# Three edits to a one-core hybrid decoder block in fp32: GpSimd's low parts of the weights in pieces, the last down product by columns, the first norm's weights spread on chip

## The chip, the cores and the metric

The kernel runs on one core of a Trainium2 chip. The metric is device time in microseconds, as the median of several runs of the whole program.

## The reference

One decoder block over 16 learned meta tokens and 256 tokens of 1024 numbers, in fp32, cut to what matters here:

```python
u = rmsnorm(h, norm_mix)                      # h: 272 x 1024
proj = u @ w_in                               # 1024 x 6160
y_ssd = ssd_branch(z, xbc, dt_raw, ...)       # Mamba-2 scan, convolution over 4 tokens
y_sc = short_conv_branch(gate_b, gate_c, hh)  # gated convolution over 3 tokens
h = h + concat(y_ssd, y_sc) @ w_out           # 2048 x 1024
u2 = rmsnorm(h, norm_ffn)
h = h + hier_moe(u2, ...)                     # 16 experts, two per token: (silu(t@Wg) * (t@Wu)) @ Wd
out = rmsnorm(h, norm_final)[:, 16:]
```

## The kernel before

The order of the instructions on each engine is the order of the code: nothing reorders it. The weights come through a ring of 22 tiles of 1 MB (`slot`), later 3 more, loaded by SP's queue in the order of use (`load`).

**Start.** SP's queue loads the meta tokens, the first 128 tokens of x in two halves, `norm_mix` twice (`gmt` for the meta tokens, `gmix` spread over 128 partitions, 512 KB), the second 128 tokens of x, the columns of dt (`wdt`) and then the tiles of `w_in`, with up to three small parameter loads (`between`) behind each. `u_squares`, `u_root` and `u_scale` make the norm of one row block, `u_turn` and `u_low` transpose it on TensorE and split it in a high part `uh` and a low part `ul`. `x_part` copies x into the four accumulators `acc[b][n]` (token block b, columns n) in PSUM, where the output product is added later.

**Projection.** `units` lists dt and 48 products of 128 columns of `w_in`. An fp32 product is made of three fast ones, (high, high), (low, high), (high, low), in `project`. `split_hi` (ScalarE, L313) and `split_lo` (L324) make a unit's weight parts two units ahead; the low part is one subtraction of 128x1024, on GpSimd for 24 of the units (`on_pool`) and on VectorE for the others. Behind a product `first` and `second` do convolution and gates on VectorE and ScalarE: L593 and L617 are taps of the convolutions, L602 and L605 gates, L504 to L515 the decay of the scan. TensorE's products use two PSUM banks ("pj") in turn, so a product waits until `first` has read the one two before.

**Experts.** Seven units, six of two experts and the last of four; each makes gate, up and down products (L1038), and its results are scattered into the accumulators (L1059). Weights are loaded when `used` frees a tile. Of the last expert tiles the second halves come in pieces: the first 1024 columns, then twice 512, for the four experts in turn (L114 to L120).

**End.** The last unit's down product makes both halves of 512 columns for each k-block in turn; then come the scatters (the first 512 columns in a high and a low part, the other 512 in fp32, L1251), the squares, the roots and the norm (`last_norm`), and six output transfers. The weights of the last norm are spread on chip in the last unit (`fin_part`, L1066).

## Time and profile before

| | |
|---|---|
| median of 3 runs | 448.89 us (448.59 to 450.16) |
| the profiled execution | 448.21 us, span 446.2 |
| busy: TensorE, VectorE, ScalarE, GpSimd | 422.9, 229.9, 159.4, 66.2 us |
| mean granted TensorE clock | 0.993 of 2.4 GHz |
| read from HBM | 138.26 MB, 312 GB/s over the span |

The span goes from the first to the last instruction of the profiled execution; the small rest lies around it. A busy time is the sum over the engine's instructions, overlaps counted once. TensorE's matmuls are pipelined and their ends are modelled, so its busy time says less than its waits do. Rows of a timeline begin with the start and the duration in us; in square brackets stands how long the engine was idle before, and what ended that.

### The profile page before, as it was taken

How to read it: one execution, taken by the hardware profiler on the slowest of the kernel's cores; microseconds unless marked ns; L12 is line 12 of the kernel's file. 1: busy time of each engine (PE TensorE's matmuls, PEld its weight loads, DVE VectorE, ACT ScalarE, POOL GpSimd, SP SyncE). 2: the span in 40 equal slices, each digit the busy share in tenths (PEclk: the TensorE clock that was granted, in tenths of full speed). 3: DMA queues.
4: the chain of work that ended last, by engine and by line, in shares of the span. 5: the costliest groups of instructions: out<-in, count | busy, mean ns of one | idle time of the engine just before them, and what ended most of it. 6: DMA issues, size and time to landing. Idle time of an engine off the chain costs nothing.

```text
span 446.2 us, 7338 instructions
## 1 busy us (share of the span) xinstructions
PE 422.9 (95%) x2905; PEld 295.3 (66%) x2905; DVE 229.9 (52%) x472; ACT 159.4 (36%) x252; POOL 66.2 (15%) x39
## 2 busy tenths in 40 slices
PE   6999999999998999999999989999999999999982
PEld 4899899999997899978878353533535335353321
DVE  5679888977896858676556621110212102122113
ACT  4675446745757345554452321010010100101113
POOL 1253324244437242100000000000000000000000
PEclk9999999999999999999999999999999999999998
DMA  7999988265699556599684799999999999999952
GB/s 201 256 272 348 348 260 291 89 188 162 208 390 385 178 189 222 182 424 387 200 298 175 309 419 413 419 419 420 418 422 416 421 419 419 420 416 421 411 202 98
DMA packets 49468, 139.85 MB, mean 313 GB/s; under 512 B 6406, under 2 KB 32918, under 8 KB 37398
## 3 DMA queue, kind: packets, MB, share of 16 engines
q1 hardware_dynamic: 49142, 138.94, 82.9%
q8 instruction: 25, 0.41, 0.4%
q10 hardware_dynamic: 288, 0.39, 0.2%
q14 instruction: 13, 0.11, 0.1%
HBM read 138.26 MB, written 1.06 MB: 312 GB/s over the span
## 4 chain that ended last, share of the span: by engine, by line
PE 75%; DVE 14%; ACT 3%; SPq 3%; DMA 2%; issue 1%; ACTq 0%; DVEq 0%
PE gu L1038 22%; PE yd L1038 11%; PE acc L345 10%; PE p_c L337 5%; PE xp L1111 4%; PE p_xs L337 3%; PE p_h L337 3%; PE acc L1059 3%; PE p_z L337 3%; PE p_b L337 3%; DVE cv L593 2%; DVE h L617 2%; DVE f L324 1%; SPq L96 1%; DMA w<-in_w_in 1%
## 5 line engine op out<-in xcount | busy, mean ns | idle before, releaser
L1038 PE MATMUL gu<-w,X 128*64 128x512 f32 (+1 forms) x512 | 100.4, 595 | 0.4 <-DVE X L1078 0.4
L313 ACT ACTIVATE f<-w 128x1024 fp32r<-128x1024 f32 x64 | 67.2, 1054 | 30.8 <-PE acc L345 13.0
L324 POOL TENSOR_TENSOR f<-w,f 128x1024 fp32r<-128x1024 f32 x24 | 60.0, 2501 | 110.1 <-ACT f L313 93.6
L1038 PEld LDWEIGHTS gu<-w,X 128*64 128x64 f32 (+1 forms) x512 | 31.1, 130 | 60.2 <-issue 58.0
L324 DVE TENSOR_TENSOR f<-w,f 128x1024 fp32r<-128x1024 f32 x40 | 50.9, 1273 | 14.7 <-ACT f L313 14.6
L1038 PE MATMUL yd<-w,hd 128*64 128x512 f32 (+1 forms) x256 | 49.6, 595 | 0.5 <-DVE hd L1048 0.5
L345 PE MATMUL acc<-f,h 128*128 128x512 f32 x192 | 44.8, 391 | 0.0
L345 PEld LDWEIGHTS acc<-f,h 128*128 128x128 f32 x192 | 35.5, 188 | 7.7 <-issue 0.4
L1208 DVE TENSOR_TENSOR hb<-hb,gu 128x512 f32<-128x512 f32 x7 | 4.8, 687 | 64.3 <-PE gu L1038 62.2
L1054 DVE SCALAR_TENSOR_TENSOR Yl<-yd,ws,Yh 128x512 fp32r<-128x512 f32 x12 | 9.0, 751 | 53.6 <-PE yd L1038 38.5
L1038 PEld LDWEIGHTS yd<-w,hd 128*64 128x64 f32 (+1 forms) x256 | 15.2, 130 | 29.2 <-issue 27.6
L1053 ACT ACTIVATE Yh<-yd,ws 128x512 fp32r<-128x512 f32 x12 | 8.3, 688 | 73.4 <-PE yd L1038 56.7
L337 PE MATMUL p_b<-uh,f 128*128 128x256 f32 x128 | 16.6, 282 | 2.6 <-DVE h L605 1.9
L1111 PEld LDWEIGHTS <-hh 128*128 128x128 bf16 x192 | 18.1, 147 | 1.6 <-issue 1.6
L1111 PE MATMUL xp<-P,hh 128*128 128x128 bf16 x192 | 19.0, 225 | 0.0
L1111 PE MATMUL xp<-P,h 128*128 128x128 bf16 x96 | 16.9, 228 | 1.7 <-ACT hb L1192 1.7
L337 PE MATMUL p_xs<-uh,f 128*128 128x272 f32 x128 | 18.0, 293 | 0.1
L337 PE MATMUL p_c<-uh,f 128*128 128x258 f32 x128 | 16.9, 284 | 1.1 <-DVE h L605 1.1
L337 PEld LDWEIGHTS p_b<-uh,f 128*128 128x128 f32 x128 | 15.6, 188 | 3.4 <-issue 3.0
L1030 ACT ACTIVATE PT<-ptp 128x256 fp32r<-128x256 f32 x7 | 2.7, 384 | 42.2 <-PE ptp L1026 42.2
L1192 ACT ACTIVATE hb<-gu 128x512 f32<-128x512 f32 x7 | 4.2, 594 | 37.0 <-PE gu L1038 37.0
L337 PE MATMUL p_h<-uh,f 128*128 128x258 f32 x128 | 16.9, 285 | 0.0
(332 smaller groups left out, 664.3 us busy)
## 6 DMA issues: line engine op xcount, KB each, us to landing
w<-in_expert_w_gate SPq DMA_DIRECT2D x32, 1024.0 KB, 12.1
w<-in_expert_w_up SPq DMA_DIRECT2D x32, 1024.0 KB, 14.2
w<-in_expert_w_down SPq DMA_DIRECT2D x28, 1024.0 KB, 12.0
w<-in_w_in SPq DMA_DIRECT2D x23, 1024.0 KB, 7.3
w<-in_w_out SPq DMA_DIRECT2D x8, 1024.0 KB, 11.4
abc<-adr SPq DMA_DIRECT2D x2, 1024.0 KB, 5.7
w<-in_expert_w_down SPq DMA_DIRECT2D x4, 512.0 KB, 16.2
w<-in_expert_w_down SPq DMA_DIRECT2D x8, 256.0 KB, 6.3
```

The lines of the kernel that those rows point to most:

```text
L313: A.activation(h, src, AF.Copy)
L324: (G if on_pool(name, c) else V).tensor_tensor(l, src, h.bitcast(F32), op=OP.subtract)
L337: T.matmul(p, st_[:, k, :], mv[:, k, t0:], start=(k == 0 and st_ is terms[0][0] and mv is uh), stop=(k == KT - 1 and mv is ul))
L345: T.matmul(acc[b][n], st_[:, 128 * b:128 * (b + 1)], mv[:, 512 * n:512 * (n + 1)], start=False, stop=False, skip_group_check=True)
L593: V.scalar_tensor_tensor(s[:, lo:], p[:, o - sh + lo:o - sh + n], cw[:, 3 - sh, ft:ft + 1], s[:, lo:], op0=OP.mult, op1=OP.add)
L617: V.scalar_tensor_tensor(y, cc[:, c, 2 - sh:258 - sh], scw[:, 2 - sh, t:t + 1], y, op0=OP.mult, op1=OP.add)
L1038: T.matmul(o[c * s:c * s + c], X[:, 128 * k + c * s:128 * k + c * s + c], ws_, start=first_, stop=last_, tile_position=(0, c * s))
L1053: A.activation(Yh, y, AF.Copy, scale=ws)
L1054: V.scalar_tensor_tensor(Yl, y, ws, Yh.bitcast(F32), op0=OP.mult, op1=OP.subtract)
L1059: T.matmul(acc[b][n], PT[:, 128 * b:128 * (b + 1)], part, start=False, stop=stop and part is Y[-1], skip_group_check=True)
L1111: T.matmul(p[:, i], hparts[j][b].rearrange("p (m k) -> p k m", k=KT)[:, 4 * q + i], P[:, b], start=(j == b == 0), stop=(j == 2 and b == 1))
L1208: V.tensor_mul(hb, hb, g)
```

## The change

- **Low parts.** Where GpSimd makes a low part, it does so in four instructions of 128x256.
- **Start.** x is loaded in two transfers of 512 KB, right behind the meta tokens; the small loads stand behind other weight tiles than before. `norm_mix` comes as 128x8 numbers (`gcol`), issued by ScalarE; VectorE makes a diagonal pattern of them and TensorE spreads it with a matrix of ones into two of the accumulators (`g_spread`), from which `u_scale` reads. The copies of x into these two (`x_part`) follow behind the first and the second product. GpSimd zeroes `f0`, which VectorE did, and some of VectorE's constants are made later.
- **End.** The last down product is made in three column pieces (`THIRDS`), with the scatters and squares of the first 512 columns between; the norm's weights are loaded spread (`fin`) behind the three tiles of the second ring; the norm takes 512 columns at a time, and ScalarE's queue issues the four output transfers.

```diff
+THIRDS = [(0, 512), (512, 256), (768, 256)]
...
-                    for a in between[:3]:
+                    few = {(0, 1): 2, (1, 0): 6}.get((j, i), 2 * (j > 5))
+                    for a in between[:few]:
                         nc.sync.dma_start(*a)
-                    del between[:3]
+                    del between[:few]
...
-    fcol = cp.tile([128, KT], F32, name="fcol")
+    fin = cp.tile([128, D], F32, name="fin")
...
-    gmix = sA[:, 0:1024]
+    gdiag, gcol, all1 = sA[:, 0:1024], sA[:, 1568:1576], sA[:, 1600:1728]
...
+    A.dma_start(gcol, raw(norm_mix, 0, [[KT, 128], [1, KT]]))
+    A.dma_start(gmt, raw(norm_mix, 0, [[0, 16], [128, 8], [1, 128]]))
     for b in range(2):
-        for n in range(2):
-            nc.sync.dma_start(xt[:, b, 512 * n:512 * n + 512], raw(x, 128 * D * b + 512 * n, [[D, 128], [1, 512]]))
-        if b == 0:
-            nc.sync.dma_start(gmt, raw(norm_mix, 0, [[0, 16], [128, 8], [1, 128]]))
-            nc.sync.dma_start(gmix, raw(norm_mix, 0, [[0, 128], [1, D]]))
+        nc.sync.dma_start(xt[:, b], raw(x, 128 * D * b, [[D, 128], [1, D]]))
     nc.sync.dma_start(wdt, raw(w_in, 3072, [[6160, 128], [128 * 6160, KT], [1, 16]]))
...
+    between += [(dtb[:16], raw(dt_bias, 0, [[1, 16], [1, 1]])), (alog, raw(A_log, 0, [[0, 128], [1, 16]]))]
     between += [(pr[a:a + n, :], row(p, n)) for p, a, n in (
         (ssd_conv_b, 0, 16), (ssd_conv_w, 16, 64), (sc_conv_w, 80, 24), (ssd_norm, 104, 8), (sc_norm, 112, 8),
         (norm_ffn, 120, 8))]
-    between += [(dtb[:16], raw(dt_bias, 0, [[1, 16], [1, 1]])), (alog, raw(A_log, 0, [[0, 128], [1, 16]])),
-                (dsk, raw(D_skip, 0, [[1, 2], [2, 8]])), (gf, raw(norm_ffn, 0, [[KT, 128], [1, KT]])),
-                (fcol, raw(norm_final, 0, [[KT, 128], [1, KT]])),
+    between += [(dsk, raw(D_skip, 0, [[1, 2], [2, 8]])), (gf, raw(norm_ffn, 0, [[KT, 128], [1, KT]])),
                 (wgr, raw(router_group_w, 0, [[4, 128], [512, KT], [1, 4]])),
...
+    V.memset(zero, 0.0)
+    f0 = slot("f0").bitcast(F32R)
+    G.memset(all1, 1.0)
+    G.tensor_copy(f0[:, 0:1024], zero.to_broadcast([128, 1024]))
...
+    def g_spread():
+        V.tensor_tensor(gdiag.rearrange("p (m k) -> p m k", k=KT), idt[:, :, None].to_broadcast([128, 128, KT]),
+                        gcol[:, None].to_broadcast([128, 128, KT]), op=OP.mult)
+        for n in range(2):
+            T.matmul(gp[n], all1, gdiag[:, 512 * n:512 * n + 512], start=True, stop=True)
+    gp = acc[0][1], acc[1][0]
     def u_squares(b):
         un[b] = un01[:, 1024 * b:1024 * b + 1024]
-        for n in range(2):
-            c = slice(512 * n, 512 * n + 512)
-            A.activation(un[b][:, c], xt[:, b, c], AF.Square, accum_out=norms[:, 3 * n + b:3 * n + b + 1])
+        A.activation(un[b], xt[:, b], AF.Square, accum_out=norms[:, 3 + b:4 + b])
     def u_root(b):
         rr[b] = r = norms[:, b:b + 1]
-        V.tensor_scalar(r, r, 1.0 / D, EPS, op0=OP.mult, op1=OP.add)
-        A.activation(r, norms[:, 3 + b:4 + b], AF.Sqrt, bias=r, scale=1.0 / D)
+        A.activation(r, norms[:, 3 + b:4 + b], AF.Sqrt, bias=eps, scale=1.0 / D)
     def u_scale(b):
         V.reciprocal(rr[b], rr[b])
         for n in range(2):
             c = slice(512 * n, 512 * n + 512)
-            V.scalar_tensor_tensor(un[b][:, c], xt[:, b, c], rr[b], gmix[:, c], op0=OP.mult, op1=OP.mult)
+            V.scalar_tensor_tensor(un[b][:, c], xt[:, b, c], rr[b], gp[n], op0=OP.mult, op1=OP.mult)
...
-        (G if on_pool(name, c) else V).tensor_tensor(l, src, h.bitcast(F32), op=OP.subtract)
+        if on_pool(name, c):
+            for k in range(0, KT, 2):
+                G.tensor_tensor(l[:, k:k + 2], src[:, k:k + 2], h[:, k:k + 2].bitcast(F32), op=OP.subtract)
+        else:
+            V.tensor_tensor(l, src, h.bitcast(F32), op=OP.subtract)
...
-    V.tensor_copy(f0, zero.to_broadcast([128, 2048]))
-    V.tensor_add(stack, idt[:32, 0:16], idt[:32, 16:32])
     t = {}
     m_sums()
+    g_spread()
     x_part(0, 0)
+    m_scale()
     u_squares(0)
     u_root(0)
-    m_scale()
-    x_part(0, 1, 0, 256)
+    u_squares(1)
+    u_root(1)
+    mean = bp.tile([128, 2, 32], F32, name="mean")
+    V.memset(mean[:, 0], 1.0 / 256)
+    V.memset(mean[:, 1], 0.0)
+    V.memset(mean[0:64, 1, 0:16], 1.0 / 64)
+    V.memset(mean[64:128, 1, 16:32], 1.0 / 64)
+    V.tensor_scalar(upper, jp, 0.0, None, op0=OP.is_ge)
+    V.tensor_scalar(nupper, jp, 0.0, -1.0, op0=OP.is_ge, op1=OP.mult)
+    V.tensor_scalar(below, jp, 0.0, None, op0=OP.is_lt)
+    sup = bp.tile([128, 128], BF, name="sup")
+    V.tensor_scalar(sup, jp, 0.0, None, op0=OP.is_gt)
+    V.tensor_add(stack, idt[:32, 0:16], idt[:32, 16:32])
     mp = m_turn()
-    x_part(0, 1, 256, 512)
     u_scale(0)
     m_low(mp)
-    u_squares(1)
-    u_root(1)
     for q in range(2):
         t[0, q] = u_turn(0, q)
-    x_part(1, 0)
     x_part(1, 1)
...
+            if i in (0, 1):
+                x_part(i, 1 - i)
...
+            nc.sync.dma_start(fin, raw(norm_final, 0, [[0, 128], [1, D]]))
...
-    def fin_part(q, tag):
-        p = bank(tag, "fp")
-        for i in range(4):
-            T.matmul(p[:, 128 * i:128 * i + 128], on1, dg[:, 4 * q + i], start=True, stop=True)
-        V.tensor_copy(fin.rearrange("p (m k) -> p k m", k=KT)[:, 4 * q:4 * q + 4],
-                      p.rearrange("p (k m) -> p k m", k=4))
...
-                    left[1, 1] = [lambda: fin_part(0, "pj")]
-                    left[1, 3] = [lambda: fin_part(1, "m")]
...
-    Y0 = [wk.tile([128, 512], F32R, name=n, tag=n) for n in ("Yh", "Yl")]
-    Y1 = ff[:, 0:512]
-    A.activation(Y0[0], ys[0], AF.Copy, scale=ws)
-    V.scalar_tensor_tensor(Y0[1], ys[0], ws, Y0[0].bitcast(F32), op0=OP.mult, op1=OP.subtract)
-    for n in range(2):
-        A.activation(Y1[:, 256 * n:256 * n + 256], ys[1][:, 256 * n:256 * n + 256], AF.Copy, scale=ws)
-    for b in range(2):
-        scatter(b, 0, PT, Y0[0:1])
+    oo = slot("o", free.pop(0)).rearrange("p (b d) -> p b d", b=2)
+    Y1 = wk.tile([128, 512], F32, name="Y1", tag="X")
+    Y = [wk.tile([128, 512], F32R, name="Yh", tag="Yh"), slot("Y", free.pop(0)).bitcast(F32R)[:, 0:512]]
+    def squares_of(b, n):
+        A.activation(oo[:, b, 512 * n:512 * n + 512], acc[b][n], AF.Square, accum_out=s4[:, b, n:n + 1])
+    for i, tag in enumerate(("m", "m", "pj")):
+        c, n = THIRDS[i]
+        y = bank(tag, "yd")[:, :n]
+        for k in range(4):
+            side_by_side(y, hd, w_of(u, 2, k, c, n), k, k == 0, k == 3)
+        if i == 0:
+            weighed(y, ws, Y)
+        elif i == 1:
+            A.activation(Y1[:, 0:256], y, AF.Copy, scale=ws)
+            for part in Y:
+                for b in range(2):
+                    scatter(b, 0, PT, [part], part is Y[1])
+            for b in range(2):
+                squares_of(b, 0)
+        else:
+            V.tensor_scalar(Y1[:, 256:512], y, ws, None, op0=OP.mult)
+    used(2 * ne)
     for b in range(2):
...
     def last_norm():
-        squares_of(0, 0)
-        first_sum(0)
-        squares_of(0, 1)
-        root(0)
-        V.reciprocal(s3[:, 0:1], s3[:, 0:1])
-        for n in range(2):
-            squares_of(1, n)
-        norm_part(0, 0, 256)
-        first_sum(1)
-        root(1)
-        norm_part(0, 256, 256)
-        norm_part(0, 512, 512)
-        V.reciprocal(s3[:, 1:2], s3[:, 1:2])
-        norm_part(1, 0, 512)
-        norm_part(1, 512, 256)
-        norm_part(1, 768, 256)
+        for b in range(2):
+            first_sum(b)
+        for b in range(2):
+            squares_of(b, 1)
+            root(b)
+        for b in range(2):
+            V.reciprocal(s3[:, b:b + 1], s3[:, b:b + 1])
+            for n in range(2):
+                c = slice(512 * n, 512 * n + 512)
+                V.scalar_tensor_tensor(oo[:, b, c], acc[b][n], s3[:, b:b + 1], fin[:, c], op0=OP.mult, op1=OP.mult)
+                A.dma_start(raw(out, b * 128 * D + 512 * n, [[D, 128], [1, 512]]), oo[:, b, c])
```

SP's queue at the start, before (`sA` and `xt` take the meta tokens, `norm_mix` and x, `w_` a tile of `w_in`, `sB`, `sC` and `dtb` small parameters):

```order
L167 DMA sA<-in_meta_tokens 128x128
L170 DMA xt<-in_x 128x512 x2
L172 DMA sA<-in_norm_mix 128x1x128
L173 DMA sA<-in_norm_mix 128x1024
L170 DMA xt<-in_x 128x512 x2
L174 DMA sB<-in_w_in 128x8x16
L92 DMA w_112<-in_w_in 128x8x128
L96 DMA sB<-in_ssd_conv_b 16x128
L96 DMA sB<-in_ssd_conv_w 64x128
L96 DMA sB<-in_sc_conv_w 24x128
L92 DMA w_112<-in_w_in 128x8x128
```

and changed:

```order
L170 DMA sA<-in_meta_tokens 128x128
L174 DMA xt<-in_x 128x1024 x2
L175 DMA sB<-in_w_in 128x8x16
L93 DMA w_110<-in_w_in 128x8x128 x2
L98 DMA dtb<-in_dt_bias 16x1
L98 DMA sC<-in_A_log 128x16
L93 DMA w_115<-in_w_in 128x8x256
L98 DMA sB<-in_ssd_conv_b 16x128
L98 DMA sB<-in_ssd_conv_w 64x128
```

Both loads of `norm_mix` have left this queue, x is whole behind the meta tokens, and the second weight tile stands ahead of the rows of `ssd_conv_b` and the like.

TensorE at the start, before (`acc_68` to `acc_71` are the accumulators, `up` the transposed norm, `p_dt` and `p_B` the first products, `prp` the transposed parameters):

```order
L251 MATMUL acc_71<-norms,sA 128x1
L271 MATMUL acc_68<-xt,idt 128x512
L271 MATMUL acc_69<-xt,idt 128x256
L261 MATMUL acc_71<-idt,sA 128x128
L271 MATMUL acc_69<-xt,idt 128x256
L279 MATMUL up<-idt,un 128x128 x8
L271 MATMUL acc_70<-xt,idt 128x512
L271 MATMUL acc_71<-xt,idt 128x512
L279 MATMUL up<-idt,un 128x128 x8
L337 MATMUL p_dt_264<-uh,f_155 128x272 x8
```

and changed:

```order
L248 MATMUL acc_71<-norms,sA 128x1
L228 MATMUL acc_69<-sA 128x512
L228 MATMUL acc_70<-sA 128x512
L268 MATMUL acc_68<-xt,idt 128x512
L258 MATMUL acc_71<-idt,sA 128x128
L276 MATMUL up<-idt,un 128x128 x8
L268 MATMUL acc_71<-xt,idt 128x512
L276 MATMUL up<-idt,un 128x128 x8
L339 MATMUL p_dt_258<-uh,f_137 128x272 x8
L339 MATMUL p_dt_258<-ul,f_137 128x272 x8
L268 MATMUL acc_69<-xt,idt 128x512
L431 MATMUL prp<-idt,sB 128x128
```

Two matmuls that spread `norm_mix` (L228) have come in ahead, and one copy of x has moved behind p_dt; another stands behind the first p_B.

TensorE in the last down product, changed, at the end of its second column piece:

```order
L1050 MATMUL yd<-w_3799,hd 32x256
L1050 MATMUL yd<-w_3801,hd 32x256
L1071 MATMUL acc_68<-Yh,PT 128x512
L1071 MATMUL acc_70<-Yh,PT 128x512
L1071 MATMUL acc_68<-Y,PT 128x512
L1071 MATMUL acc_70<-Y,PT 128x512
L1050 MATMUL yd<-w_3689,hd 32x256
L1050 MATMUL yd<-w_3691,hd 32x256
```

All four scatters of the first 512 columns stand ahead of the third piece, where they stood behind the whole product.

## Rows read from the trace of the kernel before

**Rows 1.** Two stretches: busy time by engine, granted clock, DMA share, GB/s.

```profile
9.45:12.90 3.45, 3.08 (x10) 2.44 (x11) 2.55 (x7) 2.91 (x8) 0.00 (x0) 0.51 0.72 160
...
300.00:360.00 60.00, 60.00 (x348) 25.54 (x348) 10.61 (x21) 5.14 (x9) 0.00 (x0) 1.00 1.01 419
```

**Rows 2.** TensorE's waits, 27 to 200 us: total, times, longest.

```profile
PE p_b L337 <- DVE h L605: 1.9, 1, 1.9
PE p_c L337 <- DVE h L605: 1.1, 1, 1.1
PE yp L529 <- DVE h L515: 1.0, 1, 1.0
PE p_b L337 <- DVE h L602: 0.7, 1, 0.7
PE p_B L337 <- ACT sC L611: 0.7, 1, 0.7
```

**Rows 3.** The page's group of GpSimd's low parts (busy, mean ns, idle before).

```profile
L324 POOL TENSOR_TENSOR f<-w,f 128x1024 fp32r<-128x1024 f32 x24 | 60.0, 2501 | 110.1 <-ACT f L313 93.6
```

**Rows 4.** VectorE's timeline (start, duration, line, operation, tiles, count), 128 to 140 us.

```profile
128.86 3.14 DVE L617 SCALAR_TENSOR_TENSOR h<-h,col,h 128x256 f32<-128x256 f32 x2
...
133.38 1.00 DVE L617 SCALAR_TENSOR_TENSOR h<-h,col,h 128x256 f32<-128x256 f32 x2
...
135.77 1.53 DVE L617 SCALAR_TENSOR_TENSOR h<-h,col,h 128x256 f32<-128x256 f32 x1
...
137.33 2.47 DVE L617 SCALAR_TENSOR_TENSOR h<-h,col,h 128x256 f32<-128x256 f32 x1
```

**Rows 5.** GpSimd's timeline, 134 to 141 us.

```profile
134.85 2.16 POOL L554 TENSOR_TENSOR h<-h 128x512 f32<-128x512 f32 x1 [3.66 <-ACT h L550]
136.97 2.55 POOL L324 TENSOR_TENSOR f<-w,f 128x1024 fp32r<-128x1024 f32 x1
139.49 1.46 POOL L554 TENSOR_TENSOR h<-h 128x512 f32<-128x512 f32 x1
```

**Rows 6.** GpSimd's last low part, and TensorE's product that uses it.

```profile
178.17 2.40 POOL L324 TENSOR_TENSOR f<-w,f 128x1024 fp32r<-128x1024 f32 x1 [4.81 <-ACT f L313]
...
181.42 2.06 PE L337 MATMUL p_b<-uh,f 128*128 128x256 f32 x16
```

**Rows 7.** The start: timelines of SP's queue, ScalarE, VectorE and TensorE.

```profile
5.99 4.07 SPq L96 DMA_DIRECT2D sB<-in_ssd_conv_b  x1
...
9.54 0.63 ACT L236 ACTIVATE un<-xt 128x512 f32<-128x512 f32 x1 [1.95 <-DMA xt<-in_x]
...
9.02 1.42 DVE L247 SCALAR_TENSOR_TENSOR un<-xt,norms,sA 128x512 f32<-128x512 f32 x2 [2.11 <-DMA sA<-in_norm_mix]
...
9.82 1.97 PE L279 MATMUL up<-idt,un 128*128 128x128 f32 x8 [2.11 <-DVE un L247]
...
13.94 1.04 PE L279 MATMUL up<-idt,un 128*128 128x128 f32 x8
...
15.23 1.28 PE L337 MATMUL p_dt<-uh,f 128*128 128x272 f32 x8 [0.25 <-ACT uh L280]
```

**Rows 8.** The end: TensorE, SP's last weight issue with its landing, VectorE's last.

```profile
417.55 1.16 PE L1066 MATMUL fp<-fin,o 128*128 128x128 f32 x8
...
426.13 0.33 SPq L120 DMA_DIRECT2D w<-in_expert_w_down  x1
...
w<-in_expert_w_down SPq DMA_DIRECT2D x1, 256.0 KB, 5.3
...
427.68 7.07 PE L1038 MATMUL yd<-w,hd 128*32 128x512 f32 x64 [0.52 <-DVE hd L1048]
...
434.78 0.74 PE L1059 MATMUL acc<-Yh,PT 128*128 128x512 f32 x2
...
436.85 1.02 PE L1251 MATMUL acc<-fin,PT 128*128 128x256 f32 x4
...
439.92 1.53 DVE L1258 SCALAR_TENSOR_TENSOR o<-acc,s,fin 128x512 f32<-128x512 f32 x3
```

More of the change, by code (lines that the diff above doesn't have):

```diff
@@ L210, in body @@
     V.memset(nones, -1.0)
-    f0 = slot("f0").bitcast(F32R)
     G.iota(count16, pattern=[[1, NE]], base=0, channel_multiplier=0, allow_small_or_imprecise_dtypes=True)
     G.iota(sl, pattern=[[1, CAP]], base=-1024, channel_multiplier=0, allow_small_or_imprecise_dtypes=True)
-    mean = bp.tile([128, 2, 32], F32, name="mean")
-    V.memset(mean[:, 0], 1.0 / 256)
-    V.memset(mean[:, 1], 0.0)
-    V.memset(mean[0:64, 1, 0:16], 1.0 / 64)
-    V.memset(mean[64:128, 1, 16:32], 1.0 / 64)
-    V.tensor_scalar(upper, jp, 0.0, None, op0=OP.is_ge)
-    V.tensor_scalar(nupper, jp, 0.0, -1.0, op0=OP.is_ge, op1=OP.mult)
-    V.tensor_scalar(below, jp, 0.0, None, op0=OP.is_lt)
-    sup = bp.tile([128, 128], BF, name="sup")
-    V.tensor_scalar(sup, jp, 0.0, None, op0=OP.is_gt)
     uh = up.tile([128, KT, L], F32R, name="uh")
@@ L1192, in body @@
                 A.activation(hb, g, AF.Silu)
-                if last:
-                    ff = slot("fin", free.pop(0))
-                    dg, fin = ff[:, 0:1024].rearrange("p (k m) -> p k m", k=KT), ff[:, 1024:2048]
-                    oo = slot("o", free.pop(0)).rearrange("p (b d) -> p b d", b=2)
-                    on1 = oo[:, 0, 0:128]
-                    V.memset(on1, 1.0)
-                    V.tensor_tensor(dg, idt[:, None].to_broadcast([128, KT, 128]),
-                                    fcol[:, :, None].to_broadcast([128, KT, 128]), op=OP.mult)
-                    left[1, 1] = [lambda: fin_part(0, "pj")]
-                    left[1, 3] = [lambda: fin_part(1, "m")]
                 if not last:
@@ L1219, in body @@
             P = Pn
+        if last:
+            break
         ys = [bank("m", "yd") for n in range(2)]
@@ L1222, in body @@
             for y, (c, n) in zip(ys, HALVES):
-                side_by_side(y[:, 0:n], hd, w_of(u, 2, k, c, n), k, k == 0, k == 3)
+                side_by_side(y, hd, w_of(u, 2, k, c, n), k, k == 0, k == 3)
             if k % 2:
                 used(ne)
-        if last:
-            break
         Y = weighed(ys[0], ws)
@@ L1238, in body @@
         left[0, 3] = [lambda b=b, PT=PT, k=keep: scatter(b, 1, PT, k[0]) for b in range(2)]
[L1241 to L1248 removed]
+    oo = slot("o", free.pop(0)).rearrange("p (b d) -> p b d", b=2)
[7 more added lines that the diff above has]
+        for k in range(4):
+            side_by_side(y, hd, w_of(u, 2, k, c, n), k, k == 0, k == 3)
+        if i == 0:
[10 more added lines that the diff above has]
+    used(2 * ne)
     for b in range(2):
@@ L1252, in body @@
                      Y1[:, 256 * c:256 * c + 256], start=False, stop=True, skip_group_check=True)
-            if b == 0:
-                scatter(c, 0, PT, Y0[1:], True)
-    def norm_part(b, c0, w):
-        c = slice(c0, c0 + w)
-        V.scalar_tensor_tensor(oo[:, b, c], acc[b][c0 // 512][:, c0 % 512:c0 % 512 + w], s3[:, b:b + 1], fin[:, c],
-                               op0=OP.mult, op1=OP.mult)
-        (A if c0 == 512 else nc.sync).dma_start(raw(out, b * 128 * D + c0, [[D, 128], [1, w]]), oo[:, b, c])
-    def squares_of(b, n):
-        A.activation(oo[:, b, 512 * n:512 * n + 512], acc[b][n], AF.Square, accum_out=s4[:, b, n:n + 1])
     def first_sum(b):
@@ L1293, in body @@
         over()
+        for b in range(2):
+            squares_of(b, 0)
         last_norm()
```

1 line of the change is left out of this document (removed).

## The prediction

> **What bounds the kernel now.** I read the stretches first, then who waits for whom on TensorE, then the lines behind each wait. In the expert part TensorE has no free time while the DMA engines run at 419 GB/s [rows 1]: both are full, so what follows 250 us moves only if its start moves. Before it, from 27 to 200 us, TensorE's waits are few: five of 0.7 us or more, together 5.4, every one but the last behind VectorE [rows 2]. So there are three places where time can be had: the start, these waits, and what follows the last matmul.
>
> The profiled execution takes 448.21 us (span 446.2), 0.68 under the median of the runs shown, 448.89. I make the sum against the former and take it from the latter.
>
> **GpSimd's low parts.** GpSimd makes 24 low parts of 1024 columns at 2.5 us on average [rows 3]. What they do to VectorE is in its own rows: two L617 take 1.00 us together when GpSimd is idle, 3.14 when they meet a low part, and in the next unit 1.53 for one and 2.47 for the other [rows 4]. The instruction itself needs 0.5; the rest ends when a GpSimd instruction ends (134.85 + 2.16 = 137.0 and 136.97 + 2.55 = 139.5, [rows 5]). So the two share a way into memory, and a GpSimd instruction keeps it to its end. The same rows show how it is handed over: GpSimd had its next instruction ready at 136.97 without a pause, yet the first L617 still came through by 137.30, and GpSimd's low part took 2.55 in place of 2.40 [rows 5]. A waiting VectorE instruction gets in between two GpSimd instructions.
>
> Cut into four, a piece should take 2.40 / 4 = 0.6 plus a fixed part. The row of 512 columns gives it: 1.46 against 2.40 / 2 = 1.20, at most 0.26 [rows 5]. So 0.6 to 0.86 a piece, 0.7 taken; a wait of up to 2.4 becomes one of at most 0.7 for each VectorE instruction. Then:
> - The wait of 1.9 us on L605 [rows 2] lies behind the L617 of 2.47 [rows 4]: that one falls to about 0.5 + 0.5, so 1.5 comes back there, and the earlier unit's pair (3.14) brings 1.0 more. I take all of 1.9.
> - The 0.7 on L602 lies behind the pair of 3.14: gone.
> - The 0.7 of p_B on ACT belongs to the start, below.
> - The 1.0 on L515 and the 1.1 on p_c stay. Ahead of each VectorE has a chain of instructions that read two operands from SBUF or copy within it (L496 and the twelve of L504 to L506; L566 to L568); each of them meets a piece of its own, so four short waits replace a long one and VectorE ends no sooner.
>
> That is 1.9 + 0.7, less 0.1 for what new waits take: **2.5 us**. Bounds: 0, if VectorE never gets in between, and 4.7, if the 1.0 and 1.1 go too. The Trainium skill (SBUF — State Buffer, § Who interferes with whom) says that the pair of ports is an exclusive lock for a whole instruction and that issue order decides who blocks. The hand-over in [rows 5] agrees. By that rule each piece takes the lock anew, which speaks against cutting where VectorE has a chain; the two waits that I keep are those places.
>
> GpSimd gets later itself, by 4 x 0.7 - 2.4 = 0.4 us a part. Nobody is behind it on its queue but the next part, and TensorE needs the part later: the last ends at 178.17 + 2.40 = 180.6, and its weights are used from the middle of a product that starts at 181.42, about 182.4 [rows 6]. These 1.8 us are the shortest distance of the 24, worked out in the same way; the others have 2.2 to 7.1. So this costs nothing, with 1.8 us to spare.
>
> **The start.** VectorE's first scaling of x waits 2.11 us for norm_mix, a spread read of 512 KB, and ScalarE waits 1.95 for the second half of x, which is queued behind it [rows 7]. TensorE, with nothing to do meanwhile, has its eight transposes at 1.97 us, where the same eight later take 1.04: the granted clock is 0.51 from 9.45 to 12.9 us [rows 1, 7], so mostly the lower level (1.2 GHz), after 2.11 us of idling. The change replaces the 512 KB by 128 x 8 numbers on ScalarE's queue, one VectorE product and two matmuls of 512 columns. Four records of 256 columns take 1.02 [rows 8], two records to a matmul, so 0.5 for 256 columns, 1.0 for 512 and 2 for both. They lie where TensorE has nothing else, under the landing of x. ScalarE's table load now stands behind two DMA issues; I estimate 1.5 us later than now, and ScalarE has nothing else to do before x lands.
> So the first product (15.23, [rows 7]) comes 2.1 + 0.9 = 3.0 us earlier. Two copies of 512 columns of x into the accumulators, 1.0 us each by the same row, go from the idle start into the full stream: one behind this product, one behind the next, -2.0. And the 0.7 us wait of p_B on ACT [rows 2] goes, since the queue now brings the second weight tile ahead of six small loads and not behind (one such issue stood 4.07 us, [rows 7]), and VectorE is held up less. Sum **1.7 us**. Bounds: the transposed parameter rows are now loaded behind the second tile and TensorE needs them before p_B; if they are late by all 2.0 that p_B gains, the copy and the wait leave -1.0 + 0.7 = -0.3. If the copies find room in a wait, 3.7.
>
> **The end.** The two groups that spread the last norm's weights leave TensorE (1.16 us, two such, [rows 8]); the spread read in their place, 512 KB, is queued near 186 us, where weights come tens of us before their use, and costs nothing. If that cover went it would be 0.5 MB / 419 GB/s = 1.25 us. So the last down product may start at 427.68 - 2.3 = 425.4. But its weights don't come earlier: the last transfer is issued at 426.13 and lands 5.3 us later, at 431.4, and those before it 0.63 apart each (256 KB at 419 GB/s) [rows 1, 8]. By columns, the first 512 need the last k-block's first halves, four transfers earlier: 431.4 - 4 x 0.63 = 428.9. TensorE takes 7.07 / 8 = 0.88 for a k-block of 512 columns, so would be there at 425.4 + 2.65 = 428.0 and waits 0.9. The next 256 columns need the last transfer: done at 431.4 + 0.44 = 431.9. Then four scatters of 0.37 [rows 8], hidden now under nothing (433.4), the third product 1.76 (435.1) and the four matmuls of 256 columns, 2.04: 437.1. Before, TensorE ended at 436.85 + 1.02 = 437.9.
> Behind it VectorE ended at 439.92 + 1.53 = 441.45, 3.6 later. Now the squares of the first 512 columns are done early, but all four scalings, 0.77 each, stand behind the first root. That root can follow the second of the four matmuls, 1.0 before TensorE's end, by some 1.4 (the present chain from TensorE's end to the first scaling of row block 1 is 2.0, with two squares in it): end at 437.1 - 1.0 + 1.4 + 3.1 = 440.6, 0.85 earlier. The last output is 256 KB where it was 128, 0.3 more. Together **0.6 us**. Bounds: -0.6 if the weights hold up the end by another 1.2, and 2.0 if they don't hold it up at all.
>
> Sum: 2.5 + 1.7 + 0.6 = 4.8; 448.21 - 4.8 = 443.4 for the profiled execution, 448.89 - 4.8 = **444.1** as median. What TensorE gains before 243 us moves the stream of expert weights with it, since its loads wait for the buffers that the first expert products free.
>
> **The rivals.**
> - The pieces keep the port among themselves: GpSimd's next piece starts before VectorE is let in, and VectorE waits as long as now. Then 2.5 and the 0.7 in the start stay lost: 448.89 - 1.0 - 0.6 = 447.3. Against it speaks the hand-over in [rows 5], once seen. Chance 0.13.
> - The start gives only its 0.7, because p_B waits for the parameter rows or the clock falls somewhere else: 448.89 - 0.7 - 2.5 - 0.6 = 445.1. For it speaks the issue that stood 4.07 us for no reason that I can name. Chance 0.16.
> - VectorE, less held up all along, makes up the 1.0 and 1.1 too: 444.1 - 2.1 = 442.0. Chance 0.12.
> - Slower: the pieces are dear. If one of 256 columns costs what 512 cost, 1.46 [rows 5], a part takes 5.8, ends 3.4 later, and five of the 24 distances are shorter than that: 4.2 us of new waits on TensorE, nothing gained from the port: 448.89 + 4.2 - 1.0 - 0.6 = 451.5. From 1.7 us a piece GpSimd itself would be the bound, since a part starts every 6.8 us (24 in 163). The Trainium skill (GPSIMD Engine Reference, § 3.1) lists, for each instruction, two dispatch steps in software and a wait for the slowest of eight cores, without a figure; no row here has a two-operand instruction under 512 columns. Chance 0.06.
> - My forecast: 0.53. Its own range is 442.4 to 445.8.
>
> **How the numbers follow.** 0.5%, 2.2 us, is about what a measurement of this kernel can tell from no change. Faster by more is below 446.6: forecast, start lost, more made up: 0.81. The first rival is within it: 0.13. Slower 0.06. The range goes from 441.3 (the third rival with its bound) to 447.4 (the middle of the first); it leaves out the slower case and half of the first, with the rims.
>
> **What would show it.** Right: GpSimd with 96 low parts of 0.6 to 0.75 us; no L617 over 1.3 us; the two waits on L605 and L602 gone or under 0.3, those of 1.0 and 1.1 still there; p_dt near 12, p_B near 15.5; no stretch at half clock in the first 15 us; TensorE waiting for weights inside the last down product, about 1 us twice. Wrong: VectorE instructions of 2 us and more beside GpSimd, a wait of TensorE on GpSimd, p_B not before 17, or a last down product that is fed at once.

## The result, and the profile after

The changed kernel takes 445.66 us (median of 5 runs, 445.38 to 446.34), where the kernel before, run beside it, takes 449.55 (448.59 to 450.16). The ratio is 0.9906, with a 95% interval of 0.9883 to 0.9929: 4.2 us less, between 3.2 and 5.3. The forecast was 444.1, in a range from 441.3 to 447.4, and 4.8 us less. Two executions of the kernel before, of 534 and 842 us, are left out of all that follows.

The profiled execution of the changed kernel takes 445.38 us (span 443.4), against 448.21 (446.2). These two differ by only 2.8 us. Following TensorE through both tells where:

| TensorE begins | before | changed | lead |
|---|---|---|---|
| first product (`p_dt`) | 15.23 | 11.67 | 3.6 |
| first `p_C` | 31.28 | 29.95 | 1.3 |
| first `p_z` | 76.46 | 73.77 | 2.7 |
| first `p_c` | 104.74 | 103.21 | 1.5 |
| output projection | 184.26 | 180.92 | 3.3 |
| first expert product | 243.13 | 239.80 | 3.3 |
| last down product | 427.68 | 423.37 | 4.3 |
| (VectorE ends) | 441.45 | 438.29 | 3.2 |

The lead falls in three places: between `p_dt` and `p_C`, between `p_z` and `p_c`, and in the expert part, where the two spread matmul groups that left TensorE (2 x 1.16, [rows 8]) should have brought 2.3 and brought 1.0. Each has its row below.

TensorE's waits from 27 to 200 us, which answer to [rows 2] (total, times, longest):

```profile
PE p_z L339 <- POOL f L324: 1.9, 1, 1.9
PE p_c L339 <- DVE h L607: 1.3, 1, 1.3
PE p_b L339 <- DVE h L607: 0.7, 1, 0.7
PE yp L531 <- DVE h L517: 0.5, 1, 0.5
```

The 1.9 behind VectorE has become 0.7, the 0.7 is gone, the 1.1 on `p_c` is 1.3, and the 1.0 has become 0.5 at a later unit. At the top stands a new one, on GpSimd. The group of low parts, which answers to [rows 3] (busy, mean ns, idle before):

```profile
L324 POOL TENSOR_TENSOR f<-w,f 128x256 fp32r<-128x256 f32 x96 | 82.6, 892 | 87.5 <-ACT f L310 77.7
```

892 ns is the mean, and the parts differ: thirteen of the 24 take 2.8 to 2.9 us, seven 3.0 to 3.8, three 4.5 to 5.5, and one, that of the fourth z unit, 8.6. GpSimd's timeline (start, duration) shows four pieces alone, then those of that unit:

```profile
72.00 2.83 POOL L324 TENSOR_TENSOR f<-w,f 128x256 fp32r<-128x256 f32 x4 [3.50 <-ACT f L310]
...
78.27 8.58 POOL L324 TENSOR_TENSOR f<-w,f 128x256 fp32r<-128x256 f32 x4 [3.44 <-ACT f L310]
...
79.05 3.05 POOL L324 TENSOR_TENSOR f<-w,f 128x256 fp32r<-128x256 f32 x1
...
82.06 2.39 POOL L324 TENSOR_TENSOR f<-w,f 128x256 fp32r<-128x256 f32 x1
...
84.41 2.44 POOL L324 TENSOR_TENSOR f<-w,f 128x256 fp32r<-128x256 f32 x1
```

Alone a piece takes 2.83 / 4 = 0.71 us, as estimated. In the z unit the second piece stood 3.05, and the third and fourth 2.4 each. VectorE's timeline beside the second piece is a chain of twelve instructions, each ready as the last one ends; the first and the last two, and two long ones beside the third and the fourth piece:

```profile
79.16 0.26 DVE L506 TENSOR_SCALAR h<-abc,kk 128x112 f32<-128x112 f32 x1
...
81.14 0.28 DVE L507 TENSOR_SCALAR h<-abc,kk 128x144 f32<-128x144 f32 x1
81.35 0.84 DVE L508 TENSOR_SCALAR h<-abc,kk 128x144 f32<-128x144 f32 x1
...
82.65 1.20 DVE L326 TENSOR_TENSOR f<-w,f 128x1024 fp32r<-128x1024 f32 x1
...
84.46 1.81 DVE L517 TENSOR_TENSOR h<-h,h 128x1600 f32<-128x1600 f32 x1
```

VectorE did not wait for the second piece; the piece waited for VectorE, until the twelfth (0.84 in place of 0.28) met it. The third ends 0.6 behind VectorE's own low part (L326), the fourth 0.6 behind L517. So the part was ready at 86.85 and TensorE stood for it from 85.01 on.

VectorE's side of the bargain is in the lines that answer to [rows 4] (L617 is now L619):

```profile
127.48 1.84 DVE L619 SCALAR_TENSOR_TENSOR h<-h,col,h 128x256 f32<-128x256 f32 x2
...
130.92 1.49 DVE L619 SCALAR_TENSOR_TENSOR h<-h,col,h 128x256 f32<-128x256 f32 x2
...
134.57 1.84 DVE L619 SCALAR_TENSOR_TENSOR h<-h,col,h 128x256 f32<-128x256 f32 x2
```

Pairs of 1.84, 1.49 and 1.84 us stand where 3.14, 1.00 and 1.53 + 2.47 stood.

The start, TensorE's timeline, which answers to the last part of [rows 7]:

```profile
8.41 1.04 PE L276 MATMUL up<-idt,un 128*128 128x128 f32 x8
...
13.99 1.02 PE L268 MATMUL acc<-xt,idt 128*128 128x512 f32 x2
16.02 0.30 PE L431 MATMUL prp<-idt,sB 128*128 128x128 f32 x1 [1.01 <-DMA sB<-in_norm_ffn]
16.14 2.23 PE L339 MATMUL p_B<-uh,f 128*128 128x272 f32 x16
```

The first eight transposes take 1.04 where they took 1.97, and the granted clock is 1.00 from 3 to 15 us (0.86 before). Behind the copy of x TensorE waits 1.01 for the parameter rows.

The expert part: two stretches (length, busy time and count of TensorE, its weight loads, VectorE, ScalarE and GpSimd, then granted clock, DMA share, GB/s), the changed kernel first:

```profile
256.30:259.60 3.30, 3.30 (x31) 3.25 (x29) 1.50 (x4) 0.00 (x0) 0.00 (x0) 0.51 1.01 417
```

and the kernel before, in the stretch behind the same wait:

```profile
259.20:265.20 6.00, 6.00 (x64) 4.34 (x65) 2.64 (x5) 0.15 (x1) 0.00 (x0) 1.00 1.01 415
```

In both, TensorE had waited 1.65 us ahead of the first expert's second gather (from 254.14 and from 257.47). Behind it the clock fell to its lower level (1.2 GHz) in the one execution and not in the other. From the first expert product to the last down product the changed kernel takes 423.37 - 239.80 = 183.6; before took 427.68 - 243.13 - 2.3 = 182.2.

The end: TensorE's last down product, what its weight loads waited for from 423 to 430 us, and ScalarE's queue (start, duration).

```profile
423.37 6.42 PE L1050 MATMUL yd<-w,hd 128*32 128x512 f32 x64 [0.52 <-DVE hd L1060]
429.72 0.73 PE L1071 MATMUL acc<-Yh,PT 128*128 128x512 f32 x2
```

```profile
PEld yd L1050 <- DMA w<-in_expert_w_down: 1.2, 4, 0.5
```

```profile
436.15 3.32 ACTq L1282 DMA_DIRECT2D out<-o  x4
```

The first two column pieces take 6.42, where 7.07 x 3 / 4 = 5.30 would do: 1.1 us of waiting for weights. The last output lands at 441.78, 3.5 us behind VectorE's end, where it was 444.28 - 441.45 = 2.8.

### The profile page after: what moved, and what is told of

Read it like the earlier page. It is cut to its first block, busy times and chain, and to the rows that moved or that the text cites. A ratio compares the mean times of both kernels' runs of the same rounds, so it can differ in the third digit from the quotient of the medians.

```text
span 443.4 us, 7446 instructions
## 1 busy us (share of the span) xinstructions
PE 423.8 (96%) x2923; PEld 295.0 (67%) x2923; DVE 220.3 (50%) x465; ACT 159.0 (36%) x247; POOL 89.1 (20%) x113
## 4 chain that ended last, share of the span: by engine, by line
PE 64%; DVE 7%; ACT 3%; issue 2%; POOL 1%; DVEq 0%; ACTq 0%
PE gu L1050 22%; PE yd L1050 11%; PE acc L347 10%; PE xp L1115 4%; PE p_c L339 3%; PE acc L1071 3%; PE p_h L339 3%; PE p_b L339 3%; ACT f L310 1%; PE hbp L1057 1%; DVE h L619 1%; PE xp L903 1%; DVE f L326 1%; POOL f L324 1%; DVE h L548 1%
## 5 line engine op out<-in xcount | busy, mean ns | idle before, releaser
L324 POOL TENSOR_TENSOR f<-w,f 128x256 fp32r<-128x256 f32 x96 | 82.6, 892 | 87.5 <-ACT f L310 77.7
L326 DVE TENSOR_TENSOR f<-w,f 128x1024 fp32r<-128x1024 f32 x40 | 50.6, 1264 | 17.4 <-ACT f L310 17.4
L1050 PE MATMUL yd<-w,hd 128*64 128x512 f32 (+2 forms) x288 | 50.9, 548 | 0.5 <-DVE hd L1060 0.5
L1050 PEld LDWEIGHTS yd<-w,hd 128*64 128x64 f32 (+1 forms) x288 | 16.7, 128 | 29.3 <-issue 25.5
L1115 PE MATMUL xp<-P,hh 128*128 128x128 bf16 x192 | 20.1, 232 | 0.0
L339 PE MATMUL p_z<-uh,f 128*128 128x256 f32 x128 | 17.3, 285 | 1.9 <-POOL f L324 1.9
L339 PE MATMUL p_c<-uh,f 128*128 128x258 f32 x128 | 16.8, 283 | 1.3 <-DVE h L607 1.3
L339 PEld LDWEIGHTS p_z<-uh,f 128*128 128x128 f32 x128 | 15.6, 188 | 2.4 <-POOL f L324 2.3
```

The costliest lines, as they stand in the source:

```text
L324: G.tensor_tensor(l[:, k:k + 2], src[:, k:k + 2], h[:, k:k + 2].bitcast(F32), op=OP.subtract)
L326: V.tensor_tensor(l, src, h.bitcast(F32), op=OP.subtract)
L339: T.matmul(p, st_[:, k, :], mv[:, k, t0:], start=(k == 0 and st_ is terms[0][0] and mv is uh), stop=(k == KT - 1 and mv is ul))
L1050: T.matmul(o[c * s:c * s + c], X[:, 128 * k + c * s:128 * k + c * s + c], ws_, start=first_, stop=last_, tile_position=(0, c * s))
L1115: T.matmul(p[:, i], hparts[j][b].rearrange("p (m k) -> p k m", k=KT)[:, 4 * q + i], P[:, b], start=(j == b == 0), stop=(j == 2 and b == 1))
```

## The experiments

Twelve kernels, in three sets of four; each set shares its runs of the kernel before (medians 449.62, 449.64 and 449.94). Single executions of one kernel spread by 1 to 4 us, and the reason turns out to be part of the answer. Three theories were to be told apart. **Parts**: each of the three edits gives its own share. **Clock**: waits of TensorE cost twice, since the clock falls behind some of them. **Stream**: the expert weights, at 419 GB/s without a break, set the end whatever TensorE does before.

### Each edit alone, and the pieces undone

**Four pieces alone**, on the kernel before:

```
-        (G if on_pool(name, c) else V).tensor_tensor(l, src, h.bitcast(F32), op=OP.subtract)
+        if on_pool(name, c):
+            for k in range(0, KT, 2):
+                G.tensor_tensor(l[:, k:k + 2], src[:, k:k + 2], h[:, k:k + 2].bitcast(F32), op=OP.subtract)
+        else:
+            V.tensor_tensor(l, src, h.bitcast(F32), op=OP.subtract)
```

> The kernel before with only the four-piece low parts. Theory (a waiting VectorE instruction gets in between two pieces): TensorE's waits behind the normalisation of the h units (0.7 and 1.9 us before) fall to 0.7 together, the 1.0 behind the product of the z units goes or halves, one new wait of about 1.9 us on a GpSimd piece comes in beside VectorE's chain of twelve; in all 2.0 us less, 447.5 where before is 449.5. Rival (the gain between 31 and 240 us in the changed kernel came from its earlier start, not from the pieces): 449.5, within 0.5.

Measured: 0.9978 (0.9957 to 0.9998), 1.0 us less. Its waits from 20 to 270 us are those of the changed kernel:

```profile
PE p_z L342 <- POOL f L327: 1.9, 1, 1.9
PE xp L1116 <- ACT hb L1197: 1.7, 1, 1.7
PE p_c L342 <- DVE h L610: 1.3, 1, 1.3
PE p_b L342 <- DVE h L610: 0.6, 1, 0.6
```

So the pieces gain without the new start; half of what was expected, though the waits were the expected ones. Its trace agrees with the time: from the first product to the first expert product it takes 240.85 - 14.20 = 226.7, where before took 243.13 - 15.23 = 227.9, 1.2 us less and with the clock whole in both.

**Low parts whole again**, on the changed kernel (the edit above, reversed):

> The changed kernel with GpSimd's low parts whole again (24 instructions of 1024 columns). Theory: the 2.0 us between 31 and 240 us come back, 447.7 where the changed kernel is 445.7, with VectorE instructions of 2 us and more beside GpSimd and no wait of TensorE on GpSimd. Rival (the pieces gave nothing): 445.7, within 0.5.

Measured: 0.9947 (0.9928 to 0.9965) against 0.9906 with the pieces: 1.8 us more (1.2 against the 0.9920 of the changed kernel's second set, below). The waits of 1.9 and 1.0 behind VectorE are back, and none is on GpSimd.

**The start alone**: the hunks of the diff on the start (loads, `g_spread`, `u_squares` to `u_scale`, `x_part`, `f0` and the constants), on the kernel before.

> The kernel before with only the changed start (loads, spread on the chip, copies behind the first two products). Theory: p_dt 3.5 us earlier, p_C 1.3 us earlier, with a wait of about 1.0 us for the parameter rows ahead of p_B; 1.3 us less, 448.2 where before is 449.5. If the clock falls behind the wait in the first expert's gather as it does in the changed kernel, that costs 1.3 and the time is 449.5; the trace tells which. Rival (the start is given back at a later wait): 449.5 with the clock whole.

Measured: 0.9963 (0.9942 to 0.9985), 1.7 us less. `p_dt` starts at 11.78, `p_C` at 30.19, and TensorE waits 1.1 for the parameter rows. In its profiled execution the clock fell too, but elsewhere, behind the wait of 1.93 at 137 us.

**The end alone**: the hunks on `THIRDS`, `fin` and `last_norm`, on the kernel before.

> The kernel before with only the changed end. Theory: the two groups of matmuls for the last norm's weights leave TensorE (2.3 us), 1.0 to 1.5 of it is given back in the last down product to late weights, the last output lands 0.6 later behind VectorE's end; 0.8 less, 448.7 where before is 449.5. Rival (the weights hold the end wholly, since their landing does not move): 449.5 or more, with TensorE ending no earlier than before.

Measured: 0.9965 (0.9944 to 0.9987), 1.6 us less. Its own trace can't be read for the end, since the clock fell in the expert part. The kernels below that have the same end and no fall there can: TensorE ends 193.6 to 193.8 behind the first expert product in four of them, 437.88 - 243.13 = 194.8 before. So TensorE does end sooner, by 1.0 to 1.2, and the rival falls.

The three alone come to 1.0 + 1.7 + 1.6 = 4.3, the change to 4.2. They add up, as far as intervals of about 1 us to either side each can show it.

### What the waits cost

**The changed kernel again**, as the measure of the next three.

> The changed kernel itself, for comparison with the three that are sent with it. Both theories: 445.7 where before is 449.5, a wait of 1.9 us on a GpSimd piece near 85 us, and the clock at its lower level for some 3.3 us behind the wait in the first expert's gather near 254 us.

Measured: 0.9920 (0.9896 to 0.9943). Here is the same program as in the first profile, with the same wait of 1.90 us on GpSimd near 85 us. The stretch behind it, changed kernel first:

```profile
88.00:92.00 4.00, 4.00 (x44) 3.56 (x44) 1.91 (x8) 1.33 (x2) 2.80 (x4) 1.00 0.60 168
```

and this execution:

```profile
88.00:92.00 4.00, 4.00 (x32) 3.13 (x32) 0.32 (x1) 1.33 (x2) 2.79 (x4) 0.64 0.40 96
```

44 matmuls against 32 in the same 4 us. From the first `p_z` to the first `p_c` the one takes 103.21 - 73.77 = 29.4, the other 104.80 - 73.79 = 31.0. So one fall costs 1.6 us here, and the same program has it or hasn't. All kernels with this wait agree, these two among them: 31.0 to 31.1 in four profiles with the fall, 29.4 to 29.5 in three without.

**The wait filled**: seven matmuls of 128 columns, whose result nobody reads, ahead of the gather.

```
+        for i in range(fill_):
+            T.matmul(p[:, 384:512], idt, idt, start=True, stop=True, skip_group_check=True)
...
+        PT, ws = back(P, cparts[:, :, places_of(u)], 7 if u == 0 else 0)
```

> The changed kernel with seven matmuls of 128 columns, whose result nobody reads, in the 1.65 us in which TensorE waits ahead of the first expert's second gather. Theory (the clock falls because of that wait and costs 1.3 us behind it): the granted clock stays whole from 250 to 265 us and the time falls by 1.3 to 444.4, spread less from run to run. Rival (the lower clock there is not what costs the time, or it falls all the same): 445.7, within 0.5.

Measured: 0.9901 (0.9874 to 0.9929) against 0.9920 beside it: 0.9 us less by ratio, 445.30 against 446.53 by median; the intervals overlap. The trace is plainer than the times:

```profile
256.00:260.00 4.00, 4.00 (x53) 3.98 (x52) 1.72 (x4) 1.69 (x3) 0.00 (x0) 1.00 1.01 420
```

53 matmuls at full clock, where the first profile of the changed kernel has 42 at 0.57:

```profile
256.00:260.00 4.00, 4.00 (x42) 3.95 (x40) 1.91 (x4) 0.01 (x1) 0.00 (x0) 0.57 1.01 418
```

From the first expert product to the last down product it takes 423.49 - 241.37 = 182.1, against 183.5 for the changed kernel beside it, although TensorE does seven matmuls more.

**The wait cut**: the gate function ahead of the last two conversions on ScalarE, the gathers by part (in every unit).

```
-    for b in range(2):
-        A.activation(hparts[2][b], rem[b], AF.Copy)
...
-        for i in range(4):
-            for j in range(3):
-                for b in range(2):
+        for j in range(3):
+            for b in range(2):
+                for i in range(4):
...
+                hb = wk.tile([128, 512], F32, name="hb", tag="hb0" if u == 0 else "Yh")
...
+                for b in range(2 * (u == 0)):
+                    A.activation(hparts[2][b], rem[b], AF.Copy)
```

> The changed kernel with the first expert's gate function ahead of the last two conversions of the hidden rows on ScalarE (its result in a buffer of its own), and the gathers ordered by part. Theory: the wait of 1.65 us is cut to about 0.5, the clock stays whole: 1.1 + 1.3 = 2.4 less, 443.3. Rival (the weights of the next products set the pace behind it): the wait is short and the time 445.7 all the same, with TensorE waiting for expert weights later.

Measured: 0.9907 (0.9886 to 0.9929), 445.78. The wait is wholly gone, the clock stays whole, and the last down product starts 421.46 - 241.04 = 180.4 behind the first expert product, 1.7 sooner than with the filled wait. And nothing comes of these 1.7: TensorE's weight loads in the last product wait longer (1.9, in the changed kernel's first profile 1.2),

```profile
PEld yd L1050 <- DMA w<-in_expert_w_down: 1.9, 5, 0.5
```

and TensorE ends 193.5 behind the first expert product here (434.52 - 241.04) as there (434.93 - 241.37 = 193.6): from the start of the last down product to its end it takes 13.1 here and 11.4 there. The rival was right on the late weights, the theory on the clock. The difference lies in the stream: with the fall the last weight transfer is issued 423.83 - 239.80 = 184.0 behind the first expert product (and TensorE ends 195.2 behind it), with the filled wait 182.1, with the wait cut 182.0. In these profiles a slow TensorE holds the stream up, and one that is ahead doesn't hurry it.

**One low part whole**, that of the fourth z unit:

```
+            n = 8 if (name, c) == ("z0", 3) else 2
+            for k in range(0, KT, n):
+                G.tensor_tensor(l[:, k:k + n], src[:, k:k + n], h[:, k:k + n].bitcast(F32), op=OP.subtract)
```

> The changed kernel with one of the 24 low parts whole, that of the fourth z unit, which took 8.6 us in four pieces beside VectorE's chain of twelve. Theory (in pieces it must win the way into memory four times against a queue of VectorE instructions): it takes 2.4 us again, TensorE's wait of 1.9 us on GpSimd goes and one of 1.0 behind VectorE's product of the z units comes back; 0.9 less, 444.8. Rival (whatever stands there is late, the wait only changes its name): 445.7, within 0.5.

Measured: 0.9861 (0.9836 to 0.9886), 443.60: 2.9 us less by median than the changed kernel beside it, three times what was expected (2.7 by ratio; the intervals don't meet). GpSimd's part takes 2.46 again, and the waits are as foretold:

```profile
77.66 2.46 POOL L325 TENSOR_TENSOR f<-w,f 128x1024 fp32r<-128x1024 f32 x1 [3.44 <-ACT f L310]
```

```profile
PE yp L532 <- DVE h L518: 1.4, 2, 1.0
PE p_c L340 <- DVE h L608: 1.3, 1, 1.3
PE p_b L340 <- DVE h L608: 0.7, 1, 0.7
```

0.9 us is the difference of the waits (1.90 + 0.41 in the changed kernel beside it, 1.04 + 0.38 here). From `p_z` to `p_c` the trace takes 101.36 - 73.16 = 28.2, so 1.2 less than the changed kernel without a fall there and 2.8 less than with one. The rest of the 2.9 is put down to the falls that no longer follow; that fits the clocks (0.989 to 0.996 in its five executions, 0.985 to 0.992 in the six of the changed kernel beside it), but was not measured by itself.

### Smaller questions, and all together

**Both copies of x behind the first product**:

```
-            if i in (0, 1):
-                x_part(i, 1 - i)
+            if i == 0:
+                x_part(0, 1)
+                x_part(1, 0)
```

> The changed kernel with both moved copies of x behind the first product, so that the second stands in TensorE's wait of 1.0 us for the parameter rows. Theory (that wait is for a transfer and does not move): the wait goes to 0.1, p_B starts where it did and p_C 0.9 earlier; 0.9 less, 445.2 where the changed kernel in the batch before was 446.1 by its median against before. Rival (VectorE or ScalarE behind p_B is late by as much): 446.1, within 0.5, with a wait further on.

Measured: 0.9899 (0.9867 to 0.9932), 444.81. The wait for the rows is 0.6, `p_B` starts at 15.88 and `p_C` at 28.84, 1.1 earlier than in the changed kernel, and 1.0 of this lead is still there at the output projection (179.95 against 180.92). Not all of the 1.1 is the edit's, since `p_B` starts anywhere from 15.5 to 16.8 in the nine kernels with the new start and without this edit; but from `p_B` to `p_C` it takes 12.96, also in the last kernel below, and 13.81 to 13.84 in those nine. These 0.9 us are the edit's. The time's interval is too wide to show them; the traces do.

**Outputs over two queues**:

```
-                A.dma_start(raw(out, b * 128 * D + 512 * n, [[D, 128], [1, 512]]), oo[:, b, c])
+                (A, nc.sync)[n].dma_start(raw(out, b * 128 * D + 512 * n, [[D, 128], [1, 512]]), oo[:, b, c])
```

> The changed kernel with the second half of each block's output issued by SP in place of ScalarE. Theory (the last issue stood 1.15 us on ScalarE's queue and its landing came 3.5 us after VectorE's end): the last output lands 2.8 us after VectorE's end; 0.7 less, 445.4. Rival (the transfers themselves follow one another at the memory): landing 3.3 or more after VectorE's end, 446.1, within 0.5.

Measured: 0.9906 (0.9871 to 0.9940), 445.55. The rival: the last output lands 442.20 - 438.74 = 3.5 us behind VectorE's end, as from one queue, though the last issue is over 0.4 us behind that end (439.11), where it was 1.2 (439.47 - 438.29). The last three landings are 0.5 and 0.6 apart (441.09, 441.59, 442.20). Nor does one queue need a long last issue: in three kernels (changed again, wait filled, wait cut) it is over 0.4 us behind VectorE's end too, and the last output lands 4.1 to 4.2 behind it. So the queue is not it. Why the second lands 2.1 us behind the first was not tried, but the DMA packets of the traces show what it goes with: at that time queue q8 moves a packet of 16 KB of instructions (438.08 to 439.09 in the changed kernel's first profile). In the ten kernels with this end whose landings are on record, the second output lands 1.4 to 1.6 us behind the end of that packet, and the last 2.7 behind it in nine and 2.8 in the tenth, though VectorE ends anywhere from 0.8 to 1.6 us ahead of it. Nothing here moved that packet, so the cause is not shown.

**Two pieces of 512 columns** (`n = 4` for all parts in the loop above):

> The changed kernel with the low parts in two pieces of 512 columns. Theory (a VectorE instruction waits for at most one piece, and GpSimd has to get in once for each piece): VectorE instructions beside GpSimd take up to 1.5 us more, the low part of the fourth z unit takes 5 us in place of 8.6 and TensorE's wait on it goes or falls under 0.5, the waits behind the h units come to 1.5 in place of 0.7; 0.8 less, 445.3. Rival (the pieces' number does not matter as long as there is a gap): the wait of 1.9 us stays, 446.1, within 0.5.

Measured: 0.9899 (0.9866 to 0.9932), 445.24. The z unit's part takes 4.93, TensorE does not wait for it, and the waits behind the h units come to 0.4 + 0.9:

```profile
78.83 4.93 POOL L325 TENSOR_TENSOR f<-w,f 128x512 fp32r<-128x512 f32 x2 [3.72 <-DVE h L497]
```

```profile
PE yp L532 <- DVE h L518: 1.3, 2, 1.1
PE p_c L340 <- DVE h L608: 1.1, 1, 1.1
PE p_b L340 <- DVE h L608: 0.9, 1, 0.9
...
PE p_b L340 <- DVE h L605: 0.4, 1, 0.4
```

The theory holds in each of TensorE's waits (1.3 behind the h units, 1.5 foretold); the time agrees, but its interval also holds the rival's.

**Four edits together** (one part whole, gate function first, both copies, two queues):

> The changed kernel with four of the edits together: the fourth z unit's low part whole, the gate function ahead of the conversions with the gathers by part, both copies of x behind the first product, outputs over two queues. Theory: TensorE has no wait over 1.4 us behind 20 us, so the clock stays whole to the last product; 2.9 less by the whole low part, 0.9 by the copies and 0.5 by the queues, 441.8. Rival (the stream of weights, at 419 GB/s from some 245 us, has a length of its own and eats what is gained behind its start): 442.7 or more.

Measured: 0.9821 (0.9791 to 0.9851), 441.49 (441.07 to 442.31, 6 runs): 8.0 us less than before, 3.8 less than the change. All TensorE's waits of 0.5 us and more from 20 to 420 us:

```profile
PE yp L532 <- DVE h L518: 1.5, 2, 1.0
PE p_c L340 <- DVE h L608: 1.3, 1, 1.3
PE hbp L1059 <- DVE hb L1203: 0.9, 1, 0.9
PE p_b L340 <- DVE h L608: 0.7, 1, 0.7
PE yd L1052 <- DVE hd L1062: 0.5, 1, 0.5
```

and the granted clock is 1.00 in each of four stretches over the same time, here the second and third:

```profile
140.00:260.00 120.00, 117.92 (x755) 95.18 (x755) 79.66 (x159) 54.11 (x86) 14.75 (x20) 1.00 0.74 280
260.00:380.00 120.00, 120.00 (x696) 51.05 (x694) 20.82 (x40) 10.84 (x18) 0.00 (x0) 1.00 1.01 420
```

Its six executions have clocks of 0.993 to 0.995 and lie within 1.2 us, where those of the changed kernel spread by 1.0 in the first set and 2.4 in the second. What is left is the stream: TensorE ends 430.41 - 237.40 = 193.0 behind the first expert product, 0.6 sooner than with the filled wait, though its last down product starts 1.7 sooner (180.4).

## Why the prediction was right, and where its steps failed

The direction, the size (4.2 against 4.8) and the range held. The shares by the runs were 1.0 to 1.8 (low parts), 1.7 (start) and 1.6 (end) against 2.5, 1.7 and 0.6. The first came out smaller and the last larger, so that the total is as near as it is owes something to luck.

**GpSimd's low parts (2.5).** The mechanism was right: a waiting VectorE instruction gets in between two pieces, no L619 takes over 1.1 us, the 0.7 on L602 is gone. Four things were off.
- "So this costs nothing, with 1.8 us to spare" is the step that failed. I had the pieces 0.4 us later a part, by their own duration, and counted the hand-over in one direction. It goes both ways: beside a chain that leaves no gap, each piece has to get in anew, and one part took 8.6 us, 6.1 longer than whole, where it had 3.2 us to spare in the kernel before, by the prediction's own way of reckoning. TensorE's new wait of 1.9 is as much as the sum counted for L605, and more than the 1.2 that came of it. The sentence on what would make the prediction wrong names this wait; the sum had no term for it.
- The sentence on the Trainium skill (SBUF — State Buffer, § Who interferes with whom) said that by that rule each piece takes the lock anew, and drew only the consequence for VectorE. The trace agrees with the rule; the 3.05 us of one piece is its other side.
- L605's 1.9 became 0.7, not 0: the low parts that VectorE itself makes meet pieces too (one L326 took 1.99 where 1.22 is usual).
- The 1.0 on L515 did not stay as said; it became 0.5 on a later unit. The 1.1 on `p_c` stayed, at 1.3.

The dear pieces of the slower rival are out: alone a piece takes 0.71.

**The start (1.7).** Right in sum and in its steps: `p_dt` at 11.67 (forecast near 12), no stretch at half clock, the two copies in the stream. `p_B` came at 16.14 and not 15.5, by the wait for the parameter rows that the bounds had named. Copies together show that this wait can cover one of the copies.

**The end (0.6).** Right by the traces, as far as their scatter goes. From the first expert product to the end of the span it takes 203.1 us before and 203.5 with the start alone, and 202.2 to 202.7 in four kernels with the new end and no fall in that stretch. That is some 0.4 to 1.4; the runs' 1.6 has an interval from 0.6 to 2.5. Within it:
- The wait for weights in the first two column pieces came out: 1.1, where the sum has 431.9 - 425.4 - 5.3 = 1.2. The sign "about 1 us twice" does not follow from that sum, which has 0.9 and 0.3; the trace has four short waits, 1.2 together.
- VectorE ends 1.2 to 1.4 earlier (196.9 to 197.1 behind the first expert product in those four kernels, 198.3 before) and not 0.85. This is the term that was too small.
- The 0.3 for the larger last output is neither shown nor refuted. From VectorE's end to the end of the span the old end takes 4.8, 5.2 and 6.1 (before, start alone, pieces alone), the new one 5.0 to 5.9; the 2.8 and 3.5 to the landing, above, are one execution each, and the landing goes with the packet of instructions (two queues).

**What the sum did not have.** The prediction read the clock in the first 15 us and took it as whole elsewhere, since [rows 1] show 1.00. That was one execution. In the changed kernel's profile a fall in the expert part took 1.4 us back, which is as much as the difference between the 2.8 us of the two profiles and the 4.2 by the runs' ratio: the profile of before that the prediction rested on has no fall behind 15 us and lies near the lower edge of that kernel's runs.

## What to carry to other kernels

Cutting an engine's instruction to let another in at a shared way works both ways: look on both queues for a chain without a gap, and leave the instruction whole where the other's chain is long and the result is due soon. Count the waits of TensorE by their length and not by their sum alone: here those of up to 1.3 us cost what they are, and those of 1.64 us and more may cost as much again. Where transfers run without a break to the end, as the expert weights do here, TensorE gains nothing by being early within that stretch, and being late there costs time. And one profile is one execution: compare the clocks of several before a difference of 1 or 2 us is put down to an edit.
